# A three-layer kernel on one core: modulation by feature with six open banks at the start, and reordered joints with norm products on VectorE

## The chip, the core and the metric

The kernel runs on one core of one Trainium2 chip. The metric is the device time of one launch in microseconds, in which lower is better; a kernel's time is the median of its runs. Of the core's engines the text speaks of TensorE (matrix products and transposes; PE in rows), VectorE (DVE), ScalarE (ACT), GpSimd (POOL) and SyncE (SP), whose queue issues the loads from HBM into SBUF. PSUM holds the sums of TensorE in banks of 512 floats per partition.

## The reference

Three layers over a sequence of 1024 tokens of width 1024, with a context of 256 tokens beside it. The start and the two joints matter here:

```python
def layer(x, ctx, mod_x, mod_c, norm1_w, ...):            # first layer
    sh1, sc1, g1, sh2, sc2, g2 = jnp.split(mod_x[:, None, :], 6, -1)
    csh1, csc1, ... = jnp.split(mod_c, 6, -1)
    hx = modulate(rmsnorm(x, norm1_w), sh1, sc1)          # h * (1 + scale) + shift
    hc = modulate(rmsnorm(ctx, norm1_w), csh1, csc1)
    aq, ak, av, mq, mk, mv, mo, ... = mixer_inputs(hx, w_in, ...)   # hx @ w_in, split
    ...                                                   # attention, mLSTM, w_out
    x = x + g2 * expert_choice_ffn(hx2, w_router, w_gate, w_up, w_down)

def first_block(...):
    mod_x = jax.nn.silu(c) @ w_mod[l] + b_mod[l]
    mod_c = jax.nn.silu(c_ctx) @ w_mod[l] + b_mod[l]

def even_layer(x, norm_g, w_in, ...):                     # second layer
    z = rmsnorm_2(x, norm_g) @ w_in
    ...
    return x + jnp.concatenate([y_a, y_b], axis=-1) @ w_out

def odd_layer(x, norm_g, w_in, conv_w, w_out):            # third layer
    z = rmsnorm_2(x, norm_g) @ w_in
    ...
```

All is in float32. A product of matrices is made on TensorE from operands that are split in a high part (a cast on ScalarE) and a remainder, "lo" (a subtraction on VectorE or GpSimd), as three products: high by high, low by high, high by low.

## The kernel before

**The start** (`h_all`, `mod_early`, `kv_open`, `kv_tile`). x comes in eight tiles of 128 tokens. `normed` loads a tile, squares it on ScalarE (`norm_rows`, L230), makes the reciprocal root in tiny VectorE operations (L176 to L182) and scales the rows (L358). Eight TensorE transposes (L374) and two copies bring the tile into `xnT`, where partitions are features: eight "features" kt of 128 columns, each with 1024 tokens. `mod_early` makes shift and scale for both inputs, x and context: 16 loads of 512 KB of `wmod` through the `hi` and `lo` buffers, four matmuls for each (L298) with the two columns of silu(c), a sum over all eight kt, then copies, transposes (L306), bias and scale (L307, L312). `wmod` is laid out by input kt, so that every column of shift and scale is complete only with the last load of its group of eight. `finish` then makes the modulated high part `hxh` (ScalarE, L364) and the remainder `hxl` (VectorE, L365 and L136) for half of the tokens, and `kv_tile` multiplies a token tile by the key, value and gate columns `wkv` (24 matmuls of 272 columns into one bank of `mm`, L160 to L162) and copies the result out (L418 to L420). The context follows with two tiles.

**A unit** (`unit`, L1264) multiplies normed rows by weights with seven block products where eight would be plain (sums of weight blocks, `S`, on VectorE at L1212 to L1222; sums of row blocks in `norm_pair`). Its weights come through `operands`, which loads raw blocks ahead (`feed`); `raw` has six buffers in the even joint's stretch.

**The joint into the even layer** (L1421 to L1453). The last expert matmul ends, its rows are added into `xacc` in HBM, and the rows come back as four pairs of tiles, `ph` (t and t + 4). `norm_pair` squares them, scales by the reciprocal root and by the norm's row `nrow`, transposes four quarter blocks into the banks `s` and `o` (L1321), and makes the row sums and their splits, on which `unit(…, 0)` (pairs 0 and 1) and `unit(…, 1)` (pairs 2 and 3) work with 256-column products. The third call of `unit` has 512 columns. The first tile of a pair gets one VectorE operation (L1313); the second gets a ScalarE scaling (L1314) and a GpSimd product with the row (L1315).

**The joint into the odd layer** (L1478 to L1497) is the same with the rows `x` in SBUF: the even layer's last pass adds the output to `x` (L1393), token tiles in the order 0, 4, 1, 5, 2, 6, 3, 7, and calls `then(t)` behind each, which stores the tile and after tile 5 norms pair 0, after tile 7 pair 1.

Order: a scheduler sets the order of instructions on each engine from the order of the code and priorities; `high_priority` pulls a block ahead. Within an engine, and on SyncE's queue, an instruction that waits holds all behind it.

## Time and profile before

| what | value |
|---|---|
| median of the runs | 3333.42 us (3332.51 to 3335.74, 3 runs) |
| the profiled execution | 3336.12 us, its span 3334.3 us |
| mean granted TensorE clock of the span | 0.967 of full speed |
| TensorE busy | 3098.8 us, 93% of the span |
| VectorE, ScalarE, GpSimd busy | 2026.3, 1394.8, 1206.4 us |
| TensorE's share of the chain that ended last | 41% |
| loads and stores | 366.77 MB, 110 GB/s mean |

The share of busy time is a mean over stages. Where TensorE is busy all the time, other engines' work is hidden; where it waits, the row says for whom (`<-`): the engine and the tile that ended the wait last.

### The profile page before, as it was taken

To read this page: it belongs to the slowest core of one execution; us is meant where nothing else is said; L and a number is where in the kernel's file an instruction comes from. 1 tells how busy PE (TensorE), PEld (TensorE's weight loads), DVE (VectorE), ACT (ScalarE), POOL (GpSimd) and SP (SyncE) were. 2 spreads that over 40 slices of the span, in tenths; PEclk is the share of its full clock that TensorE was granted. 3 is DMA by queue.
4 is the path that set the end of the run, shared out by engine and by line. 5 is a ranking of instruction groups with operands and counts; after the bars stand their busy time and mean duration, and the time that the engine had idled before them with its cause. 6 is when DMAs were issued, how large, how long until landed. Compare 5 with 4: busy or idle time off the path is not lost. (4 is left out here: it accounts for less than half of the span.)

```text
span 3334.3 us, 43810 instructions
## 1 busy us (share of the span) xinstructions
PE 3098.8 (93%) x15829; PEld 2559.3 (77%) x15829; DVE 2026.3 (61%) x3879; ACT 1394.8 (42%) x2564; POOL 1206.4 (36%) x855
## 2 busy tenths in 40 slices
PE   6998988997999689999997999999999999999998
PEld 5986765775777577888785888888888888777787
DVE  5886678666999755455556455455455455444545
ACT  5645465444877542333314433333333333233312
POOL 0000000001332455455744434334334333666663
PEclk8998989998999899999998999999999999999999
DMA  5344223329999412221621111111111111211342
GB/s 199 96 138 129 62 75 115 98 96 392 371 378 366 111 39 73 76 70 64 205 82 63 47 45 51 45 48 48 45 51 45 47 49 45 69 64 64 110 149 76
DMA packets 142878, 366.77 MB, mean 110 GB/s; under 512 B 17299, under 2 KB 27059, under 8 KB 142661
## 3 DMA queue, kind: packets, MB, share of 16 engines
q1 hardware_dynamic: 137764, 346.14, 30.2%
q0 software_dynamic: 4896, 17.83, 2.1%
q8 instruction: 125, 2.05, 0.3%
q14 instruction: 93, 0.75, 0.1%
HBM read 311.43 MB, written 52.48 MB: 109 GB/s over the span
## 5 line engine op out<-in xcount | busy, mean ns | idle before, releaser
L1264 PE MATMUL ps_mm<-h,hi 128*128 128x512 f32 (+1 forms) x4272 | 1088.6, 394 | 44.7 <-ACT qk L1292 10.8
L1264 PEld LDWEIGHTS ps_mm<-h,hi 128*128 128x128 f32 x4272 | 784.2, 189 | 215.3 <-ACT qk L1292 17.2
L134 POOL TENSOR_TENSOR lo<-S,hi 128x512 fp32r<-128x512 f32 x302 | 402.9, 1337 | 586.9 <-PE ps_mm L1264 398.4
L1264 PE MATMUL ps_mm<-h,lo 128*128 128x512 f32 (+1 forms) x2136 | 566.6, 388 | 0.0
L1264 PEld LDWEIGHTS ps_mm<-h,lo 128*128 128x128 f32 x2136 | 399.7, 189 | 82.5
L134 POOL TENSOR_TENSOR lo<-raw,hi 128x512 fp32r<-128x512 f32 (+1 forms) x244 | 337.4, 1387 | 313.0 <-ACT hi L1196 232.8
L1196 ACT CAST hi<-S 128x512 fp32r<-128x512 f32 x302 | 187.1, 620 | 531.7 <-PE ps_mm L1264 510.9
L136 DVE TENSOR_TENSOR lo<-raw,hi 128x1024 fp32r<-128x1024 f32 (+1 forms) x218 | 285.0, 1330 | 35.5 <-ACT hi L148 31.7
L1196 ACT CAST hi<-raw 128x512 fp32r<-128x512 f32 x240 | 148.9, 622 | 369.5 <-PE ps_mm L1264 323.1
L148 ACT CAST hi<-raw 128x1024 fp32r<-128x1024 f32 (+1 forms) x222 | 230.8, 1050 | 96.0 <-PE ps_mm L162 60.7
L1217 DVE TENSOR_TENSOR S<-raw,raw 128x512 f32<-128x512 f32 x76 | 66.6, 877 | 202.7 <-POOL lo L134 201.5
L323 POOL MEMSET macc<- 128x512 f32 x8 | 4.2, 526 | 474.3 <-DMA mods<-macc 354.6
L160 PE MATMUL ps_mm<-hi,hxh 128*128 128x256 f32 (+1 forms) x448 | 131.6, 296 | 3.0 <-ACT hxh L364 2.8
L162 PE MATMUL ps_mm<-hi,hxl 128*128 128x256 f32 (+1 forms) x448 | 129.4, 292 | 2.4 <-DVE hxl L136 2.3
L161 PE MATMUL ps_mm<-lo,hxh 128*128 128x256 f32 (+1 forms) x448 | 130.8, 293 | 0.0
L1213 DVE TENSOR_TENSOR S<-S,raw 128x512 f32<-128x512 f32 x76 | 103.7, 1364 | 39.2 <-POOL lo L134 38.9
L161 PE MATMUL ps_mm<-lo,xT 128*128 128x512 f32 x256 | 105.3, 411 | 15.1 <-DVE lo L136 12.7
L1183 POOL TENSOR_TENSOR y<-y,g 128x1024 f32<-128x1024 f32 x15 | 40.2, 2679 | 198.9 <-ACT y L1179 178.7
L1294 DVE TENSOR_TENSOR qk<-ps_mm,pq 128x512 f32<-128x512 f32 (+1 forms) x75 | 69.1, 938 | 68.9 <-PE ps_mm L1264 68.6
L1745 DVE CUSTOM_DVE_ANT_0 P<-ps_s,bias 128x128 f32<-128x128 f32 (+1 forms) x192 | 61.8, 348 | 80.4 <-PE ps_s L1740 78.9
L160 PE MATMUL ps_mm<-hi,xT 128*128 128x512 f32 x256 | 103.8, 405 | 2.4 <-ACT hi L148 2.1
L1365 ACT CAST yh<-r 128x1024 fp32r<-128x1024 f32 x28 | 29.4, 1050 | 180.5 <-PE ps_s L161 168.5
(587 smaller groups left out, 6430.4 us busy)
## 6 DMA issues: line engine op xcount, KB each, us to landing
raw<-in_wexp_dram SPq DMA_DIRECT2D x192, 512.0 KB
raw<-in_wo_dram SPq DMA_DIRECT2D x228, 256.0 KB
mraw<-in_wmod_dram SPq DMA_DIRECT2D x64, 256.0 KB
raw<-in_we_dram SPq DMA_DIRECT2D x64, 256.0 KB
r<-ye SPq DMA_DIRECT2D x14, 512.0 KB
r<-in_weo_dram SPq DMA_DIRECT2D x14, 512.0 KB
r<-yo SPq DMA_DIRECT2D x14, 512.0 KB
r<-in_wo_dram SPq DMA_DIRECT2D x14, 512.0 KB
```

Of the source, the lines that this page charges most:

```text
L134: nc.gpsimd.tensor_sub(lo, raw, hi.bitcast(F32))
L136: nc.vector.tensor_sub(lo, raw, hi.bitcast(F32))
L148: self.nc.scalar.copy(hi, raw)
L160: nc.tensor.matmul(out, l[0], r[0], start=start, stop=False)
L161: nc.tensor.matmul(out, l[0], r[1], start=False, stop=False)
L162: nc.tensor.matmul(out, l[1], r[0], start=False, stop=stop)
L1196: self.nc.scalar.copy(hi, x)
L1213: nc.vector.tensor_sub(s2, s1, a11)
L1217: nc.vector.tensor_sub(s3, a11, a21)
L1264: nc.tensor.matmul(ps, w[a][:, kt * P:(kt + 1) * P], h[b][:, kt, cs], start=start and i == 0, stop=i == 11, skip_group_check=True)
L1294: self.nc.vector.tensor_add(dst, ps, add)
L1745: nc.vector.tensor_tensor_reduce(p, ps, bias[:, n - m:], op0=ALU.add, op1=ALU.max, scale=1.0, scalar=-3e38, accum_out=mx[:, j:j + 1])
```

## The change

It has three parts.

1. **Start.** The host lays `wmod`'s first two groups out by output feature (`wmodf`): two loads of 512 KB bring all inputs for the shift and the scale of one feature. `mod_sum(f)` sums them on TensorE with silu(c) in 32-column weights (`cpad`), `mod_cols(f, …)` turns the row into columns with two small products by a selector `sel`. So features get ready one by one. The key and value banks of six token tiles (three of `mm`, three of `g`) are opened together, and `step(kt, nxt)` adds feature kt to all six: modulation of tokens 0 to 768, the sums of feature `nxt` = kt + 2, 12 matmuls of the first two terms, `mod_cols(nxt)`, 6 matmuls of the third. Tiles 6 and 7 come in after steps 2 and 4, and their keys and values follow behind the six. The loads' and TensorE's order is written by hand (`manual_schedule`). x tiles take other buffers (`X2`, `hi`, `lo`, three of `hx`).
2. **Norm products.** Both tiles of a pair get the VectorE operation; `norm_pair` becomes a generator with a stop between norm and transposes.
3. **Joints.** Even: on SyncE `nrow` and the eight first raw loads go ahead of the ph loads, pairs 0 and 1 are normed before either is transposed, pairs 2 and 3 are loaded and normed ahead of unit 0. Odd: pairs 0 to 3 are normed after tiles 4, 5, 6 and 7 and pairs 0 and 1 transposed after 6 and 7; the odd output weights' first four raw blocks are loaded at tile 0 (`self.early`).

```diff
-    def mod_early(self):
...
+    def mod_open(self):
...
+        self.cpad = self.t("cpad", [KT, 32])
+        nc.gpsimd.memset(self.cpad, 0.0)
+        nc.vector.tensor_copy(self.cpad[:, :, 0:2], self.csil.rearrange("p a k -> p k a"))
+        self.sel = self.t("sel", [2])
+        nc.vector.tensor_reduce(self.sel, self.ident.rearrange("p (j x) -> p x j", j=4)[:, 0:2], axis=AX.X, op=ALU.add)
...
+    def mod_load(self, f):
+        self.wm[f] = [self.t("X", [4, 256], name="wm") for _ in range(2)]
+        for h in range(2):
+            self.nc.sync.dma_start(self.wm[f][h].rearrange("p a b -> p (a b)"), self.A["wmodf"][f][:, h * D:(h + 1) * D])
+    def mod_sum(self, f):
+        nc = self.nc
+        ps = self.pt("tr")
+        for h in range(2):
             for j in range(4):
+                nc.tensor.matmul(ps[32 * j:32 * j + 32, :256], self.cpad[:, 4 * h + j], self.wm[f][h][:, j],
+                                 start=h == 0, stop=h == 1, tile_position=(0, 32 * j))
+        return ps
+    def mod_cols(self, f, ps):
+        nc = self.nc
+        row = self.t("hrow", [2, P])
+        nc.scalar.copy(row.rearrange("p a b -> p (a b)"), ps[:, :256])
+        pw = self.pt("tr")
+        for i in range(2):
+            nc.tensor.matmul(pw[:, 2 * i:2 * i + 2], row[:, i], self.sel, start=True, stop=True)
+        nc.vector.tensor_add(self.modc.rearrange("p a (i f) -> p f i a", i=2)[:, f], pw[:, 0:4].rearrange("p (i a) -> p i a", i=2),
+                             self.col("bmod")[:, 0:16].rearrange("p (i f) -> p f i", i=2)[:, f, :, None].to_broadcast([P, 2, 2]))
+        nc.vector.scalar_tensor_tensor(self.sc1[:, :, f], self.modc[:, :, 8 + f], 1.0, self.col("n1")[:, f:f + 1].to_broadcast([P, 2]),
+                                       op0=ALU.add, op1=ALU.mult)
...
+        spare = [self.t("hx", [D], name="xin") for _ in range(3)]
         self.hx = ([self.t("hx", [D], F32R, "hxh") for _ in range(KT)], [self.t("hx", [D], F32R, "hxl") for _ in range(KT)])
...
+        xt, self.wm, self.pre = {}, {}, []
+        self.mod_open()
+        with self.tc.manual_schedule(engines={nc.sync.engine, nc.tensor.engine}):
+            def loads(text):
+                for what in text.split():
+                    i = int(what[1])
+                    if what[0] == "x":
+                        xt[i] = rows("x", i, tile=spare[i - 5] if i > 4 else None,
+                                     tag=("xin", "xin", "X2", "hi", "lo")[min(i, 4)])
...
+                    elif what[0] == "m":
+                        self.mod_load(i)
...
+                        self.pre.append(self.wraw(A["wkv"][i]))
+            def part(f):
+                self.mod_cols(f, self.mod_sum(f))
+            def step(kt, nxt):
+                for s in (slice(0, 512), slice(512, 768)):
+                    finish(self.hx[0][kt][:, s], self.hx[1][kt][:, s], xnT[:, kt, s], kt, 0)
+                sums = self.mod_sum(nxt) if nxt < KT else None
+                for t in range(6):
+                    self.kv_part(ps[t], t, kt, (0, 1))
+                if sums is not None:
+                    self.mod_cols(nxt, sums)
+                for t in range(6):
+                    self.kv_part(ps[t], t, kt, (2,))
+            loads("x0 x1 m0 x2 x3 w0 m1 x4 x5 w1 m2")
+            tile_in(0)
+            tile_in(1)
+            part(0)
+            self.wkv = self.wpair(A["wkv"])
+            tile_in(2)
+            tile_in(3)
+            part(1)
+            tile_in(4)
+            tile_in(5)
+            ps = [self.pt(("mm", "g")[t // 3]) for t in range(6)]
+            loads("m3")
+            step(0, 2)
+            loads("x6 m4")
+            step(1, 3)
+            loads("m5")
+            step(2, 4)
+            tile_in(6)
+            loads("x7 m6")
+            step(3, 5)
+            loads("m7")
+            step(4, 6)
+            tile_in(7)
+            self.pre += [self.wraw(A["wcv"][0][i]) for i in range(2)]
+            step(5, 7)
+            step(6, 8)
+            step(7, 8)
         self.kv_open()
+        for t in range(6):
+            self.kv_out(ps[t], t)
+        s = slice(768, 1024)
+        for kt in range(KT):
+            finish(self.hx[0][kt][:, s], self.hx[1][kt][:, s], xnT[:, kt, s], kt, 0)
+        for t in (6, 7):
+            self.kv_tile(t)
+        hc = [self.t("X", [4, 256], F32R, "hc") for _ in range(4)]
+        self.hc = ([hc[k // 4][:, k % 4, :] for k in range(KT)], [hc[2 + k // 4][:, k % 4, :] for k in range(KT)])
+        ts = normed([rows("ctx", t) for t in range(2)])
         for kt in range(KT):
             ps = self.pt("tr")
...
+    def kv_part(self, ps, t, kt, terms=(0, 1, 2)):
+        hx = self.hx if t < 8 else self.hc
+        s = slice(t % 8 * P, t % 8 * P + P)
+        for i in terms:
+            self.nc.tensor.matmul(ps[:, :272], hx[i == 2][kt][:, s], self.wkv[i == 1][kt], start=kt == i == 0,
+                                  stop=kt == KT - 1 and i == 2)
+    def kv_out(self, ps, t):
...
+        def load(i, j):
+            if self.early:
+                return self.early.pop(0)
+            return self.wraw(srcs[i][:, j * 512:(j + 1) * 512]) if i < n else None
...
     def feed(self, srcs, tiles):
-        pairs = [(x[:, 0], x[:, 1]) for x in (self.spare(t) for t in tiles)]
+        pairs = [(x[:, 0], x[:, 1]) for x in tiles]
...
-        nc.vector.scalar_tensor_tensor(xn[0], xs[0], rs[:, 0:1], row, op0=ALU.mult, op1=ALU.mult)
-        nc.scalar.mul(xn[1], xs[1], rs[:, 1:2])
-        nc.gpsimd.tensor_mul(xn[1], xn[1], row)
+        for i in range(2):
+            nc.vector.scalar_tensor_tensor(xn[i], xs[i], rs[:, i:i + 1], row, op0=ALU.mult, op1=ALU.mult)
+        yield
         ps = {}
         for n, bank in zip(("11", "12", "22", "21"), banks):
...
         out("T2", t2, "pool")
         out("B21", ps["21"], "dve")
         out("T4", t4, "pool")
+        yield
...
-            self.feed([A["we7"][i // 5 * 4 + i % 5 - 1] if i % 5 else self.wf[i // 5] for i in range(20)], ("q", "q", "s"))
-            row = self.t("s", [D], name="nrow")
-            nc.sync.dma_start(row, A["en"].to_broadcast([P, D]))
-
-            def norm(t):
+            def load(t):
                 x = xs[t] if t < 2 else two("ph")
                 for i in range(2):
                     nc.sync.dma_start(x[i], self.xacc[(t + 4 * i) * P:(t + 4 * i + 1) * P, :])
...
+                return self.norm_pair(t, x, row, T, ("s", "o", "s", "o"))
+            def step(*ts):
                 with self.tc.high_priority(offset=100):
-                    self.norm_pair(t, x, row, T, ("s", "o", "s", "o"))
-
-            norm(0)
-            norm(1)
+                    for t in ts:
+                        next(n[t])
+            with self.tc.manual_schedule(engines={nc.sync.engine}):
+                pairs = [self.spare(t) for t in ("q", "q", "s")]
+                row = self.t("s", [D], name="nrow")
+                nc.sync.dma_start(row, A["en"].to_broadcast([P, D]))
+                self.feed([A["we7"][i // 5 * 4 + i % 5 - 1] if i % 5 else self.wf[i // 5] for i in range(20)], pairs)
+                n = [load(t) for t in range(2)]
+            step(0, 1, 0, 1)
+            n += [load(t) for t in (2, 3)]
+            step(2, 3)
             for a in tl:
                 nc.gpsimd.memset(a[:, 0:16], 0.0)
             self.unit(self.put2(tl, 16), None, 0)
-            norm(2)
-            norm(3)
+            step(2, 3)
             self.unit(self.put2(tl, 16, 1), None, 1)
...
-                def norm(t):
+                n = [self.norm_pair(t, [self.xs[t], self.xs[t + 4]], row, lambda i: self.t("T", [512]), ("s",) * 4)
+                     for t in range(4)]
+                def step(*ts):
                     with self.tc.high_priority(offset=100):
-                        self.norm_pair(t, [self.xs[t], self.xs[t + 4]], row, lambda i: self.t("T", [512]), ("s",) * 4)
+                        for t in ts:
+                            next(n[t])
...
                 def then(t):
+                    if t == 0:
+                        self.early = [self.wraw(A["wo7"][0][:, j * 512:(j + 1) * 512]) for j in range(4)]
                     nc.sync.dma_start(self.x3d[t * P:(t + 1) * P, :], self.xs[t])
-                    if t in (5, 7):
-                        norm((t - 5) // 2)
+                    if t in (4, 5):
+                        step(t - 4)
+                    elif t > 5:
+                        step(t - 6, t - 4)
                 self.out_sums(A["weo"], self.ye, [((15,), (0, 4, 1, 5, 2, 6, 3, 7), then)], ("o",))
-                self.feed([A["wo7"][i] for i in range(56)], ("X",) * 3)
+                self.feed([A["wo7"][i] for i in range(56)], [self.spare("X") for _ in range(3)])
                 self.qk = [self.t("qk", [D]) for _ in range(2)]
                 self.unit(self.put2(self.qk), None, 0)
-                norm(2)
-                norm(3)
+                step(2, 3)
                 self.unit(self.put2(self.qk, 0, 1), None, 1)
...
-    a["wmod"] = np.stack([chunk(wm[:, j * D:(j + 1) * D]) for j in range(6)])
+    a["wmod"] = np.stack([chunk(wm[:, j * D:(j + 1) * D]) for j in range(2, 6)])
+    a["wmodf"] = np.stack([chunk(np.concatenate([wm[:, i * D + k * P:i * D + k * P + P] for i in range(2)], 1)) for k in range(8)])
```

Three places show what this moves. **TensorE, end of the modulation**, before (`hi`, `lo` hold `wmod` and then `wkv`, `ps_mm` the banks):

```order
L298 MATMUL ps_mm_394<-lo_425,csil 2x256 x4
L298 MATMUL ps_mm_394<-hi_431,csil 2x256 x4
L298 MATMUL ps_mm_394<-lo_437,csil 2x256 x4
L374 MATMUL ps_tr_237<-ident,xin_224 128x128 x4
L374 MATMUL ps_tr_243<-ident,xin_224 128x128 x4
L306 MATMUL ps_g_449<-ident,hrow_443 128x128
L306 MATMUL ps_g_452<-ident,hrow_443 128x128
L160 MATMUL ps_mm_513<-hi_460,hxh_93 128x272
L161 MATMUL ps_mm_513<-lo_461,hxh_93 128x272
L160 MATMUL ps_mm_541<-hi_460,hxh_93 128x272
```

and now (`wm` holds a feature's weights, `ps_mm` and `ps_g` the six banks, `hxh_96` is feature 0):

```order
L387 MATMUL ps_tr_329<-ident,xin_93 128x128 x4
L387 MATMUL ps_tr_335<-ident,xin_93 128x128 x4
L310 MATMUL ps_tr_359<-wm_147,cpad_115 32x256 x4
L310 MATMUL ps_tr_359<-wm_148,cpad_115 32x256 x4
L490 MATMUL ps_mm_341<-hi_217,hxh_96 128x272
L490 MATMUL ps_mm_341<-lo_218,hxh_96 128x272
L490 MATMUL ps_mm_342<-hi_217,hxh_96 128x272
L490 MATMUL ps_mm_342<-lo_218,hxh_96 128x272
L490 MATMUL ps_mm_343<-hi_217,hxh_96 128x272
L490 MATMUL ps_mm_343<-lo_218,hxh_96 128x272
```

The sums of one feature stand directly ahead of the products of another, and a feature is used in six banks before the next one comes.

**SyncE's queue, even joint**, before (`wf` and `we` are the unit's raw weights, `xacc` the rows, `en` the norm's row):

```order
L140 DMA raw_10841<-in_we_dram 128x512
L140 DMA raw_10843<-in_we_dram 128x512
L1432 DMA ph_10826<-xacc 128x1024
L1432 DMA ph_10827<-xacc 128x1024
L1432 DMA ph_10828<-xacc 128x1024
L1432 DMA ph_10829<-xacc 128x1024
L140 DMA raw_10863<-in_we_dram 128x512
L140 DMA raw_10875<-in_we_dram 128x512
L140 DMA raw_11243<-in_we_dram 128x512
L140 DMA raw_11245<-in_we_dram 128x512
L1427 DMA nrow_10879<-in_en_dram 128x1024
L140 DMA raw_11305<-in_we_dram 128x512
```

and now:

```order
L1540 DMA nrow_10911<-in_en_dram 128x1024
L140 DMA raw_10913<-wf 128x512
L140 DMA raw_10915<-wf 128x512
L140 DMA raw_10917<-wf 128x512
L140 DMA raw_10919<-wf 128x512
L140 DMA raw_10921<-in_we_dram 128x512
L140 DMA raw_10923<-in_we_dram 128x512
L140 DMA raw_10943<-in_we_dram 128x512
L140 DMA raw_10955<-in_we_dram 128x512
L1518 DMA ph_10902<-xacc 128x1024
L1518 DMA ph_10903<-xacc 128x1024
L1518 DMA ph_10904<-xacc 128x1024
```

The norm's row moved from behind the ph loads to the head, and the last two of eight raw loads moved ahead of the ph loads.

**VectorE, odd joint, pairs 2 and 3** (`pq` and `qk` are the sums of unit 0's products, `T` and `h` the row sums and remainders), before:

```order
L1294 TENSOR_TENSOR qk_15923<-ps_mm_15926,pq_15979 128x256
L1294 TENSOR_TENSOR qk_15923<-ps_mm_15925,pq_15979 128x256
L1294 TENSOR_TENSOR qk_15922<-ps_mm_15926,pq_15953 128x256
L176 TENSOR_SCALAR rst_16027<-ss_16021 128x2
L178 RECIPROCAL rst_16027<-rst_16027 128x2
L179 TENSOR_TENSOR rst_16027<-rst_16027 128x2
L180 TENSOR_TENSOR rst_16027<-rst_16027 128x2
L181 TENSOR_SCALAR rst_16027<-rst_16027 128x2
L182 TENSOR_TENSOR ss_16022<-rst_16027 128x2
L1313 SCALAR_TENSOR_TENSOR x_3074_14419<-x_3074_14419,ss_16022,row_15639 128x1024
L176 TENSOR_SCALAR rst_16087<-ss_16081 128x2
L178 RECIPROCAL rst_16087<-rst_16087 128x2
```

and now:

```order
L182 TENSOR_TENSOR ss_15890<-rst_15895 128x2
L1429 TENSOR_TENSOR T_15962<-ps_s_15942,T_15948 128x512
L1306 TENSOR_TENSOR S_16287<-raw_15989,raw_16011 128x512
L1403 SCALAR_TENSOR_TENSOR x_3100_14494<-x_3100_14494,ss_15890,row_15714 128x1024
L1403 SCALAR_TENSOR_TENSOR x_3101_14495<-x_3101_14495,ss_15890,row_15714 128x1024
L176 TENSOR_SCALAR rst_15976<-ss_15970 128x2
L136 TENSOR_TENSOR h_15702<-ps_s_15937,h_15701 128x4x128
L136 TENSOR_TENSOR h_15700<-ps_s_15942,h_15699 128x4x128
L178 RECIPROCAL rst_15976<-rst_15976 128x2
L179 TENSOR_TENSOR rst_15976<-rst_15976 128x2
L180 TENSOR_TENSOR rst_15976<-rst_15976 128x2
L181 TENSOR_SCALAR rst_15976<-rst_15976 128x2
```

The norm of pair 2 moved ahead of unit 0's sums, between the remainders of pair 1, and a second product with `row` follows the first.

## Rows read from the trace of the kernel before

**Rows 1.** page, part 1: busy us, share of the span, instructions

```profile
PE 3098.8 (93%) x15829; PEld 2559.3 (77%) x15829; DVE 2026.3 (61%) x3879; ACT 1394.8 (42%) x2564; POOL 1206.4 (36%) x855
```

**Rows 2.** by stretch: engines' busy us (instructions), clock, DMA share, GB/s

```profile
0.00:10.00 10.00, 0.88 (x8) 0.14 (x8) 1.86 (x9) 5.17 (x8) 0.71 (x6) 1.00 0.78 272
...
20.00:30.00 10.00, 6.85 (x50) 2.68 (x50) 3.90 (x18) 4.92 (x12) 0.32 (x1) 0.54 1.03 416
...
60.00:70.00 10.00, 9.86 (x80) 9.64 (x79) 7.61 (x19) 7.10 (x13) 0.00 (x0) 1.00 0.17 52
```

**Rows 3.** waits of TensorE, 0 to 120 us: total us, times, longest

```profile
PE ps_mm L298 <- DMA hi<-in_wmod_dram: 15.0, 4, 9.1
```

**Rows 4.** TensorE by time, start: start us, us, instruction, count, [idle before]

```profile
31.37 0.61 PE L298 MATMUL ps_mm<-lo,csil 128*2 128x256 f32 x8
...
36.36 1.03 PE L298 MATMUL ps_mm<-lo,csil 128*2 128x256 f32 x8 [1.94 <-DMA lo<-in_wmod_dram]
...
43.72 0.59 PE L160 MATMUL ps_mm<-hi,hxh 128*128 128x272 f32 x1 [2.75 <-ACT hxh L364]
```

**Rows 5.** ScalarE in order of time, end of the start

```profile
89.91 0.44 ACT L418 COPY kc<-ps_mm 128x128 f32<-128x128 f32 x2 [2.23 <-PE ps_mm L162]
```

**Rows 6.** ScalarE by line and shape, to 100 us: busy us, mean ns

```profile
L364 ACT ACTIVATE hxh<-xnT,modc,sc 128x512 fp32r<-128x512 f32 x16 | 11.7, 803 | 1.1 <-DVE sc L312 1.0
```

**Rows 7.** VectorE by line and shape, 0 to 100 us

```profile
L136 DVE TENSOR_TENSOR hxl<-tmp,hxh 128x512 fp32r<-128x512 f32 x16 | 10.5, 688 | 0.0
L365 DVE TENSOR_SCALAR tmp<-xnT,sc,modc 128x512 f32<-128x512 f32 x16 | 8.2, 543 | 0.0
```

**Rows 8.** TensorE in order of time, even joint

```profile
1149.68 1.09 PE L1321 MATMUL ps_s<-ident,ph 128*128 128x128 f32 x4 [24.81 <-DVE ph L1313]
...
1158.82 1.79 PE L1264 MATMUL ps_mm<-h,hi 128*128 128x256 f32 x7 [1.24 <-DVE h L136]
...
1175.50 0.68 PE L1321 MATMUL ps_s<-ident,ph 128*128 128x128 f32 x4 [4.26 <-DVE ph L1313]
1178.72 1.11 PE L1321 MATMUL ps_o<-ident,ph 128*128 128x128 f32 x4 [2.54 <-POOL ph L1315]
...
1188.11 1.10 PE L1264 MATMUL ps_mm<-h,hi 128*128 128x256 f32 x7 [1.31 <-DVE h L136]
...
1195.96 1.32 PE L1264 MATMUL ps_mm<-h,hi 128*128 128x512 f32 x5
```

**Rows 9.** SyncE's queue in order of time, even joint

```profile
1132.33 1.94 SPq L1432 DMA_DIRECT2D ph<-xacc  x4
...
1140.50 0.42 SPq L1427 DMA_DIRECT2D nrow<-in_en_dram  x1
```

**Rows 10.** VectorE in order of time, even joint

```profile
1126.89 7.59 DVE L1217 TENSOR_TENSOR S<-raw,raw 128x512 f32<-128x512 f32 x1
...
1142.68 0.16 DVE L182 TENSOR_TENSOR ss<-rst 128x2 f32<-128x2 f32 x1
...
1148.26 2.47 DVE L1313 SCALAR_TENSOR_TENSOR ph<-ph,ss,nrow 128x1024 f32<-128x1024 f32 x2
```

**Rows 11.** TensorE in order of time, odd joint

```profile
1794.30 1.11 PE L1321 MATMUL ps_s<-ident,x 128*128 128x128 f32 x4 [6.09 <-DVE h L136]
...
1820.70 0.77 PE L1321 MATMUL ps_s<-ident,x 128*128 128x128 f32 x4 [4.26 <-DVE x L1313]
1823.92 1.97 PE L1321 MATMUL ps_s<-ident,x 128*128 128x128 f32 x8 [2.45 <-POOL x L1315]
...
1834.78 1.86 PE L1264 MATMUL ps_mm<-h,hi 128*128 128x256 f32 x7 [0.72 <-DVE h L136]
...
1843.68 1.55 PE L1264 MATMUL ps_mm<-h,hi 128*128 128x512 f32 x6
```

**Rows 12.** VectorE in order of time, odd joint

```profile
1787.27 0.68 DVE L1393 TENSOR_TENSOR x<-x,ps_o 128x512 f32<-128x512 f32 x1
...
1788.62 2.25 DVE L1313 SCALAR_TENSOR_TENSOR x<-x,ss,row 128x1024 f32<-128x1024 f32 x1
```

## Prediction before the run

> **What bounds the kernel now.** I read the engines' shares first: TensorE is busy 93% of the span [rows 1], so most of the program runs at TensorE's own pace, and an edit off that path is worth nothing. The edits touch three stretches where TensorE is not at that pace: the start (0 to 90 us), the joint into the even layer (1124 to 1196 us) and the joint into the odd layer (1781 to 1844 us). I read each by itself: busy time by stretch, then TensorE's waits and its instructions in order of time, then the engine that released them.
>
> In the start the loads run at 272 GB/s in the first 10 us and at 416 later [rows 2]. TensorE has little to do meanwhile: from 20 to 30 us it is 6.85 us busy, at a mean granted clock of 0.54, near the lower of its two levels (1.2 GHz). Its longest wait is for the tiles of `wmod`, 15.0 us in 4 waits [rows 3]. The last `wmod` sum begins at 36.36 [rows 4]; only behind it can any column of shift and scale be made, and the first key and value product starts at 43.72, after 2.75 us of waiting for ScalarE's first modulated tile. From 60 us TensorE runs 80 matmuls in 10 us, 0.125 us each, at a clock of 1.00 [rows 2]. The context's keys are copied out at 89.91 [rows 5]; behind that the program goes on as before, so I measure the start by that row.
>
> In the even joint TensorE idles 24.81 us until the first normed pair is there, and later 4.26 us for VectorE's product of the second half and 2.54 us for GpSimd's [rows 8]. The odd joint looks the same: 6.09, then 4.26 and 2.45 us [rows 11].
>
> **The change part by part. Start.** The stream up to the third feature's weights is six x tiles and two context tiles (0.52 MB each), two `wkv` tiles (0.56) and three features (1.05 each): 8.5 MB with the small constants. 2.7 MB arrive by 10 us; the rest at 416 GB/s takes 14 us, so the last bytes land at 24 us at best. The first step cannot start before: its first instructions on TensorE are the sums of feature 2. I take 26.5.
>
> A step is 18 matmuls of 0.125 us (2.25), eight sums in two groups of 0.61 (1.22) [rows 4] and two small ones that turn rows into columns (0.2, an estimate, since a 272-column one is 0.125): 3.7 us. Beside it VectorE has a 512-wide modulation and remainder, 0.54 + 0.69 [rows 7], and about half of that again for the 256-wide ones, 2.2 us with the columns; ScalarE has 0.80 [rows 6], its half and a copy. So TensorE bounds a step if the loads hold. The four weight buffers hold two features, and each reload is released by the sums two steps ahead: a load of 2.5 us at 416 GB/s, its latency and an x tile now and then have 7.4 us. That fits, with little left.
>
> Eight steps are 29.6 us. I give 2 us to the lower clock at their beginning, and 1 us each to the transposes of tiles 6 and 7. The six banks close at 26.5 + 29.6 + 2 + 2 = 60.1. Then come 48 matmuls for tiles 6 and 7 (6.0 us), whose modulation (eight 256-wide slices on VectorE) hides only in part, 2 us; 16 context transposes (2 us), 48 matmuls (6.0). And here is a wait that key products used to cover: the context's norm and modulation now stand behind the copies out of the banks on ScalarE and VectorE, with no other work left on TensorE: 1 to 3 us, I take 2. That is 78.1; I take 77, since the first of tile 6's products can run under the last slices. 77 is 13 us before 89.91. Bounds: 18 us if the steps begin at 24 at the full clock and nothing is uncovered, 2 if every step waits for its load.
>
> **Even joint.** The ph loads were issued at 1132.33 and `nrow` only at 1140.50, behind four raw loads and their waits for buffers [rows 9]. The row came last: the first pair's reciprocal root was there at 1142.68 + 0.16, its product began at 1148.26 [rows 10]. Now `nrow` goes first. But two raw loads that stood behind the ph loads stand ahead of them now, and their buffers come free when VectorE's sum of L1217 ends, at 1126.89 + 7.59 = 1134.48 [rows 10]; four ph loads are queued behind that on SP and go out at about 1134.9, 2.5 us later. Issue to root took 10.5 us, so the root is there at 1145.4 and two products of 1.24 end at 1147.9: TensorE starts some 2 us before 1149.68. The second pair's products end by 1151.4. From there to the second unit's first operand VectorE has 24 half-row sums and remainders (0.69 [rows 7]), four products, five quarter-size sums (0.4, an estimate from the same row) and a dozen tiny ones (0.16 in [rows 10]): 16.6 + 5.0 + 2.0 + 2.0 = 25.6, so 1177. It was 1188.11 [rows 8]. TensorE's own sum says the same: unit 0 took 12.4 us (1158.82 to 1175.50 less its wait of 4.26), 32 transposes take 5.4 to 8.7 (0.68 or 1.09 for four). Gain 11, so the 512-wide unit begins at 1185, not 1195.96; what ends late then is VectorE. What can uncover the cost: ScalarE's squares of the third pair now stand ahead of casts of the first, so if that pair's loads are late, the first unit waits with them, 2 to 4 us. Bounds 4 and 15.
>
> **Odd joint.** Nothing is loaded here but the row. The pairs start a tile earlier, and pairs 2 and 3 are normed under unit 0 and not after it, so the waits of 4.26 and 2.45 us and the slow transposes around them go [rows 11]. VectorE bounds: its last addition began at 1787.27 [rows 12], and with one product more ahead of it ends near 1789. To the second unit's first operand it then has 19 sums and remainders (13.1), six products (7.4), four operand sums of weights (2.8), five quarter-size ones (2.0) and 18 tiny ones (2.9): 28.2, so 1817, and 1818.5 with some waiting, against 1834.78 [rows 11]. TensorE has less than that there (12.4 + 5.4 us to the same point). Gain 16, the 512-wide unit at 1827.5; bounds 10 and 20.
>
> **Norm products.** They are inside these sums: each adds 1.24 us to VectorE and takes a multiplication off ScalarE and one off GpSimd. VectorE instructions on two SBUF tiles are stretched at times: L1217 to 7.59 us [rows 10], a product to 2.25 [rows 12]. The Trainium skill (SBUF — State Buffer, section Who interferes with whom) says that a VectorE instruction with two SBUF inputs contends with a GpSimd instruction that reads SBUF, and that issue order decides who is blocked. By that rule the added products are of the very kind that can be held, which speaks against this edit; what it would cost is the second rival. The two stretched rows agree with it.
>
> The rest of the program keeps its instructions; loads that change places in other stages I put at 0, within 2 us either way.
>
> **Sum.** 13 + 11 + 16 = 40 us. The profiled execution of before took 3336.12 us, of which 3334.3 are its span; that is 2.7 above the median of the runs. So 3296 in a profile, 3293 as the median.
>
> **The rivals.** *The loads pace the start.* For it: the whole stream of the start is 14.9 MB, which at 416 GB/s cannot end before 39 us, and the weight buffers are two features deep. Against it: 2.5 us of load stand against 3.7 us of step. It would leave 2 of the 13 us: 3304.
> *GpSimd holds the added products.* Eight products each pay 1.0 us more (2.25 less 1.24 [rows 10, 12]), and the remainders queued behind them on VectorE pay with them; with 4 us for squares that wait for late ph loads, 12 of the joints' 27 us go: 3305. For it: VectorE is what I expect to be late next. Against it: GpSimd loses four multiplications per joint, and its queue is shorter.
> *TensorE stays at 1.2 GHz (slower than before).* Place: the eight steps and the first two units of both joints, whose work now comes in smaller pieces with waits between. At the lower level a matmul is 0.25 us; a step is 6.5 (18 of these and the sums at some 1.0 a group), 52 us from 26.5, and 28 more for tiles 6 and 7 and the context: the start ends at 106.5, 17 us late. A unit would lose 10 us, four of them 40, more than the 27 the joints gain. Together 30 us slower: 3363. It decides if the granted clock from 30 to 60 us stays near 0.5; in the old start it was 1.00 once matmuls ran without gaps [rows 2], so I hold it unlikely.
> *The first two together*: 3316.
>
> **How the numbers follow.** Forecast 0.62 (by itself 3283 to 3300), loads 0.14, products 0.14, these two together 0.06, half clock 0.04. A measurement of this kernel can tell about 0.2% (6.7 us) from no change; of the two together I give 0.02 to a gain within that. Faster 0.94, same 0.02, slower 0.04. The range begins where all three parts gain their most (18 + 15 + 20 = 53 us, 3280) and ends at 3313, above each single rival and below the two together.
>
> **What would show it.** Right: the first key products near 27 us, steps 3.7 us apart, a granted clock above 0.9 from 35 us, the context copy near 77. The ph loads go out some 10 us after the last expert matmul, TensorE idles there 22 to 23 us, no later wait in the joint is over 2 us, and the 512-wide unit begins 60 us after the last expert matmul, not 71. In the odd joint the 512-wide unit begins some 38 us after the last addition, not 56. Wrong: a wait for `wm` above 1 us in every step; many products above 2 us; a granted clock of 0.5 through the units; a new wait in a stage that the change does not touch.

## The result and the profile after

The changed kernel takes 3307.94 us (median of 4 runs, 3305.60 to 3310.66), the kernel before 3334.58 beside it (4 runs): ratio 0.9915, interval 0.9901 to 0.9928. By these medians it is 26.6 us faster, by the ratio 28.3; forecast were 40. The time lies in the range, but 15 us above the forecast, where two of the rivals had theirs (3304 and 3305), so the terms have to be gone through.

The profile after, span and clock of the core:

```profile
core 0: 3305.9 us, clock 0.972
```

I cut the program at four marks that both traces have: the copy of the context's keys on ScalarE, the end of the last expert matmul, the first 512-wide matmul of the even layer's units (`ps_mm<-h,hi`, 128x512), and the same in the odd layer. Times in us from the span's start.

| | before | after | gain to here |
|---|---|---|---|
| context keys copied | 89.91 | 83.47 | 6.4 |
| last expert matmul ends | 1124.86 | 1112.32 | 12.5 |
| even 512-wide unit begins | 1195.96 | 1177.19 | 18.8 |
| odd 512-wide unit begins | 1843.68 | 1814.22 | 29.5 |
| span | 3334.3 | 3305.9 | 28.4 |

By the terms of the sum: start 12.5 (forecast 13, though only 6.4 of it where I looked for it), even joint 71.10 to 64.87, 6.2 (11), odd joint from the first x transpose 62.28 to 50.52, 11.8 (16), and 2.1 lost in what lies between and after the joints (0). Each figure is from one profile. Kernels below whose even joint has the same source lie up to 2.2 us apart there (63.55 to 65.75), those with the same odd joint up to 1.5 (50.51 to 52.01), s3 apart, so a difference of less than some 2 us is not shown by one mark alone.

**Start.** Busy time by stretch (us; PE, PEld, DVE, ACT, POOL with instructions; then TensorE's granted clock, DMA share, GB/s), against [rows 2]:

```profile
20.00:30.00 10.00, 7.41 (x41) 5.29 (x40) 8.39 (x24) 6.03 (x12) 0.00 (x0) 0.50 0.90 329
30.00:40.00 10.00, 9.90 (x99) 7.57 (x98) 7.83 (x25) 6.13 (x12) 0.00 (x0) 0.98 0.72 251
```

TensorE in order of time there (start, length, instruction; in brackets the idle time before it and what ended it), against [rows 4]:

```profile
17.22 1.01 PE L321 MATMUL ps_tr<-sel,hrow 128*128 128x2 f32 x4 [1.81 <-ACT hrow L318]
18.09 1.95 PE L387 MATMUL ps_tr<-ident,xin 128*128 128x128 f32 x8
21.58 1.94 PE L387 MATMUL ps_tr<-ident,xin 128*128 128x128 f32 x8 [1.54 <-DVE rst L176]
23.45 1.94 PE L310 MATMUL ps_tr<-wm,cpad 128*32 128x256 f32 x16
26.44 1.01 PE L321 MATMUL ps_tr<-sel,hrow 128*128 128x2 f32 x4 [1.05 <-ACT hrow L318]
27.31 3.60 PE L387 MATMUL ps_tr<-ident,xin 128*128 128x128 f32 x16
31.01 1.07 PE L310 MATMUL ps_tr<-wm,cpad 128*32 128x256 f32 x16
32.01 0.39 PE L490 MATMUL ps_mm<-hi,hxh 128*128 128x272 f32 x1
...
34.92 1.07 PE L310 MATMUL ps_tr<-wm,cpad 128*32 128x256 f32 x16
```

The first step begins at 31.01, not at 26.5, and what stands before it is not a load: from 10 us on no wait of TensorE ends with one, and from 15 to 31 us none of ScalarE or VectorE either. Between 20 and 30 us TensorE is 7.41 us busy at a granted clock of 0.50 (1.2 GHz) with transposes and sums of 1.94 us a group, and waits in between for ScalarE's row copy and VectorE's root: each x tile goes in turn through VectorE, TensorE and ScalarE. From there the steps are 3.91 us apart.

Behind the steps the context, on ScalarE. The second row here is the copy of tile 6's and 7's keys, the last the context's:

```profile
65.78 1.06 ACT L230 ACTIVATE junk<-xin 128x1024 bf16<-128x1024 f32 x1 [2.33 <-DVE hxl L136]
...
69.69 0.43 ACT L496 COPY kx<-ps_mm 128x128 f32<-128x128 f32 x2 [1.29 <-PE ps_mm L490]
...
72.39 1.02 ACT L377 ACTIVATE hc<-ps_tr,modc,sc 128x256 fp32r<-128x256 f32 x2 [2.26 <-PE ps_tr L466]
...
83.47 0.43 ACT L496 COPY kc<-ps_mm 128x128 f32<-128x128 f32 x2 [1.98 <-PE ps_mm L490]
```

What TensorE does between these two copies (69.70 to 83.45) besides the context's 48 products is 16 transposes, with one wait for VectorE's scaled rows, and 24 products of the next stage's weights with `hc`, nearly all of which stand ahead of the last key product (groups: busy us, mean ns of one | idle before):

```profile
L466 PE MATMUL ps_tr<-ident,xin 128*128 128x128 f32 x16 | 2.7, 281 | 1.8 <-DVE xin L371 1.8
L160 PE MATMUL ps_mm<-hi,hc 128*128 128x256 f32 x8 | 2.2, 281 | 0.0
```

**Even joint**, TensorE in order of time, against [rows 8]: the idle stretch behind the experts is 21.54 us, not 24.81; unit 0's first product begins at 1144.76, 32.4 us after the last expert matmul as in the kernel before, the third pair's second tile comes late (1155.11), and unit 1's first full product starts only at 1169.50.

```profile
1111.93 0.39 PE L162 MATMUL ps_mm<-hi,aT 128*128 128x512 f32 x1
1133.86 1.09 PE L1410 MATMUL ps_s<-ident,ph 128*128 128x128 f32 x4 [21.54 <-DVE ph L1403]
...
1144.76 2.59 PE L1353 MATMUL ps_mm<-h,hi 128*128 128x256 f32 x8 [0.98 <-ACT h L1416]
...
1155.11 1.11 PE L1410 MATMUL ps_s<-ident,ph 128*128 128x128 f32 x4 [1.54 <-DVE ph L1403]
...
1169.50 1.10 PE L1353 MATMUL ps_mm<-h,hi 128*128 128x256 f32 x7 [1.28 <-DVE h L136]
...
1177.19 1.09 PE L1353 MATMUL ps_mm<-h,hi 128*128 128x512 f32 x4
```

VectorE between, against [rows 10]: the same kinds of instruction quiet (to 1136.25) and beside GpSimd (from 1146.13). A pair of products takes 2.48 or 3.96 us, an operation on two numbers 0.16 or 1.2. GpSimd's rows stand below them.

```profile
1131.83 0.16 DVE L180 TENSOR_TENSOR rst<-rst 128x2 f32<-128x2 f32 x1
1132.03 0.17 DVE L181 TENSOR_SCALAR rst<-rst 128x2 f32<-128x2 f32 x1
...
1132.43 2.48 DVE L1403 SCALAR_TENSOR_TENSOR ph<-ph,ss,nrow 128x1024 f32<-128x1024 f32 x2
...
1146.87 1.20 DVE L180 TENSOR_TENSOR rst<-rst 128x2 f32<-128x2 f32 x1
1148.10 1.21 DVE L181 TENSOR_SCALAR rst<-rst 128x2 f32<-128x2 f32 x1
...
1151.10 3.96 DVE L1403 SCALAR_TENSOR_TENSOR ph<-ph,ss,nrow 128x1024 f32<-128x1024 f32 x2
```

```profile
1146.77 1.29 POOL L134 TENSOR_TENSOR h<-g,h 128x512 fp32r<-128x512 f32 x1
1148.01 1.28 POOL L134 TENSOR_TENSOR h<-PT,h 128x512 fp32r<-128x512 f32 x1
```

The two small operations end at 1148.07 and 1149.31, GpSimd's two subtractions at 1148.06 and 1149.29: each small operation is held until its neighbour's instruction ends. From 1130.2 to 1144.3 GpSimd does nothing, and there the same operations take 0.16.

**Odd joint**, TensorE, against [rows 11]: the waits of 6.09, 4.26 and 2.45 us have become 8.14 and 2.64. In the 8.14 us four small operations of VectorE took 3.4 (0.80, 0.75, 0.71 and 1.18), where 0.65 is their quiet time.

```profile
1777.97 1.11 PE L1410 MATMUL ps_s<-ident,x 128*128 128x128 f32 x4 [8.14 <-DVE x L1403]
...
1785.80 0.58 PE L1353 MATMUL ps_mm<-h,hi 128*128 128x256 f32 x1 [2.64 <-ACT h L1416]
...
1814.22 1.09 PE L1353 MATMUL ps_mm<-h,hi 128*128 128x512 f32 x4
```

### The profile page after: what moved, and what is told of

It reads as the page before. It is cut to its first block, busy times and chain, and to the rows that moved or that the text cites. A ratio compares the mean times of both kernels' runs of the same rounds, so it can differ in the third digit from the quotient of the medians.

```text
span 3305.9 us, 43866 instructions
## 1 busy us (share of the span) xinstructions
PE 3084.2 (93%) x15857; PEld 2552.1 (77%) x15857; DVE 2034.8 (62%) x3915; ACT 1385.7 (42%) x2564; POOL 1186.9 (36%) x846
## 4 chain that ended last, share of the span: by engine, by line
PE 75%; DVE 10%; DMA 7%; ACT 4%; issue 3%; POOL 1%; SPq 0%; DVEq 0%; ACTq 0%; POOLq 0%
PE ps_mm L1353 42%; PE ps_mm L161 4%; PE ps_mm L162 4%; PE ps_mm L160 4%; PE ps_o L1918 2%; DVE lo L136 2%; DMA raw<-in_wexp_dram 2%; PE ps_s L1845 2%; PE ps_s L162 1%; PE ps_s L160 1%; PE ps_s L161 1%; ACT hi L148 1%; PE ps_s L1901 1%; PE ps_tr L1033 1%; PE ps_O L1040 1%
## 5 line engine op out<-in xcount | busy, mean ns | idle before, releaser
L1306 DVE TENSOR_TENSOR S<-raw,raw 128x512 f32<-128x512 f32 x76 | 59.7, 786 | 202.9 <-POOL lo L134 201.7
L161 PE MATMUL ps_mm<-lo,xT 128*128 128x512 f32 x256 | 104.6, 409 | 15.6 <-DVE lo L136 14.2
L161 PE MATMUL ps_mm<-lo,hxh 128*128 128x256 f32 x384 | 111.2, 290 | 0.0
L162 PE MATMUL ps_mm<-hi,hxl 128*128 128x256 f32 x384 | 111.0, 290 | 0.0
L160 PE MATMUL ps_mm<-hi,hxh 128*128 128x256 f32 x384 | 110.5, 290 | 0.0
```

The source lines that it names most:

```text
L160: nc.tensor.matmul(out, l[0], r[0], start=start, stop=False)
L161: nc.tensor.matmul(out, l[0], r[1], start=False, stop=False)
L162: nc.tensor.matmul(out, l[1], r[0], start=False, stop=stop)
```

## Experiments

All marks of all kernels, each from its own profile (us). "Even" is from the last expert matmul to the 512-wide unit, "odd" from the first x transpose to the 512-wide unit, "unit to unit" from the one 512-wide unit to the other.

| kernel | median, ratio [95%] | context copy | expert end | even | odd | unit to unit |
|---|---|---|---|---|---|---|
| before | | 89.91 | 1124.86 | 71.10 | 62.28 | 647.7 |
| after | 3307.94, 0.9915 [0.9901, 0.9928] | 83.47 | 1112.32 | 64.87 | 50.52 | 637.0 |
| s1_start | 3321.01, 0.9958 [0.9944, 0.9971] | 85.31 | 1111.64 | 69.46 | 61.46 | 646.1 |
| s2_even | 3329.77, 0.9982 [0.9973, 0.9991] | 90.53 | 1123.48 | 63.55 | 61.81 | 648.3 |
| s3_odd | 3328.07, 0.9978 [0.9969, 0.9987] | 89.78 | 1122.30 | 70.17 | 54.29 | 640.7 |
| s4_norm | 3333.30, 0.9995 [0.9986, 1.0004] | 91.05 | 1123.98 | 69.10 | 61.57 | 645.5 |
| c1_oldprod | 3308.16, 0.9904 [0.9886, 0.9922] | 86.47 | 1109.20 | 64.60 | 55.96 | 641.4 |
| c2_tiny | 3295.32, 0.9869 [0.9852, 0.9885] | 86.71 | 1111.31 | 62.55 | 47.58 | 631.2 |
| c3_ctx | 3311.40, 0.9918 [0.9901, 0.9935] | 84.63 | 1115.17 | 65.75 | 52.01 | 637.8 |
| c4_wkv | 3306.46, 0.9913 [0.9896, 0.9930] | 84.87 | 1110.28 | 65.40 | 50.51 | 637.2 |
| c5_pool | 3303.32, 0.9900 [0.9883, 0.9916] | 83.63 | 1110.46 | 66.76 | 51.04 | 635.5 |
| c6_act | 3330.99, 0.9991 [0.9981, 1.0000] | 84.61 | 1109.99 | 64.60 | 47.75 | 639.7 |
| c8_ph | 3301.02, 0.9901 [0.9884, 0.9917] | 87.10 | 1110.70 | 62.86 | 50.53 | 635.7 |
| c7_best | 3321.92, 0.9959 [0.9944, 0.9973] | 86.27 | 1113.76 | 57.15 | 51.68 | 641.4 |

### One part of the change at a time

Each kernel is the one before with one part of the diff ahead of the prediction: s1 the whole of the start and nothing else, s2 the even joint with its order and its second product on VectorE, s3 the same for the odd joint, s4 the old orders with only this, in both joints:

```diff
-        nc.vector.scalar_tensor_tensor(xn[0], xs[0], rs[:, 0:1], row, op0=ALU.mult, op1=ALU.mult)
-        nc.scalar.mul(xn[1], xs[1], rs[:, 1:2])
-        nc.gpsimd.tensor_mul(xn[1], xn[1], row)
+        for i in range(2):
+            nc.vector.scalar_tensor_tensor(xn[i], xs[i], rs[:, i:i + 1], row, op0=ALU.mult, op1=ALU.mult)
```

> The kernel before with the new start alone; both joints stay as they were. In the trace of the changed kernel the context keys are copied out 6.4 us earlier than before, but the last expert matmul ends 12.5 us earlier, so some 6 us more come from the stretch between, whose code is the same. Theory A (the start also shifts what follows it, by the order and the loads that it leaves behind): this kernel is 11 to 14 us faster than before, about 3322, and its last expert matmul is 12 us earlier. Theory B (the 6 us belong to the run or to the other edits): it is 6 us faster, about 3328, and its last expert matmul 6 us earlier.

Measured: 14.0 us faster by the ratio (before took 3336.4 beside it). The context's copy comes 4.6 us earlier, the last expert matmul 13.2. So more than half of the start's worth appears behind the stage that was changed, with neither joint touched. Much of it appears in the head and attention stage. Busy time from 450 to 510 us, before and then s1_start (columns as above):

```profile
450.00:510.00 60.00, 52.49 (x278) 40.22 (x278) 51.67 (x207) 39.83 (x118) 0.53 (x1) 0.77 0.15 45
```

```profile
450.00:510.00 60.00, 51.19 (x309) 38.34 (x310) 51.73 (x216) 42.36 (x116) 0.00 (x0) 0.89 0.10 32
```

309 matmuls instead of 278 in the same 60 us, at a clock of 0.89 instead of 0.77, though the two windows do not hold quite the same piece of work. All ten kernels with the new start show 0.87 to 0.90 there, the four with the old one 0.77 to 0.80. The source of that stage is the same; the schedule is not: TensorE's order differs in dozens of places. That the other order raises the clock is argued, not shown, since no kernel here has the old start with the new order.

> The kernel before with the even joint alone (order of loads and norms, both products on VectorE there); start and odd joint as before. Theory A (the parts add up, and the joint is worth what the changed kernel's trace shows between the last expert matmul and the 512-wide unit, 65.0 us against 71.1): 6 us faster, about 3328.5. Theory B (the joint gains the 11 us that I forecast, and the changed kernel lost part of it only together with the other edits): about 3323.5.

Measured: 6.0 us faster by the ratio, 7.6 in the joint itself. That is theory A; the 11 us are not there when the joint stands alone either.

> The kernel before with the odd joint alone (order of norms, early raw loads, both products on VectorE there). Theory A (parts add up; in the changed kernel the 512-wide unit begins 42.4 us after the last addition, 56.4 before, of which 2 are lost ahead of that addition): 11 to 12 us faster, about 3323. Theory B (the 16 us that I forecast are there when the joint stands alone): about 3318.5.

Measured: 7.3 us faster by the ratio, 8.0 in the joint. That is neither theory: two thirds of the 11.8 us of the changed kernel. The joint's source is the changed kernel's, the new products too, so no run explains the 3.8 us between them.

> The kernel before with nothing but the second product of each pair moved from ScalarE and GpSimd to VectorE; all orders as before. Theory A (the waits of 2.5 us for GpSimd's product go, and where GpSimd's subtractions run, VectorE's new products are stretched, but none ends later than GpSimd's did): 2.5 us in the even joint and 3 to 4 in the odd one, 5 to 7 us faster, about 3328.5. Theory B (the products are held by GpSimd long enough to take that back): within 2 us of before, with products of 2 to 4 us in the trace.

Measured: no difference that the runs can tell; the joints are 2.0 and 0.7 us shorter, no more than such a mark scatters. By their ratios s1, s2 and s3, which hold s4's products in their joints, sum to 14.0 + 6.0 + 7.3 = 27.3 us, and the whole has 28.3: the parts neither help nor hinder one another much.

### What the joints pay for

c1 is the changed kernel with the old product of a pair's second tile (ScalarE, then GpSimd). c2 leaves the refinement of the reciprocal root out of the norms of both joints: the root is ScalarE's alone. c1:

```diff
-        for i in range(2):
-            nc.vector.scalar_tensor_tensor(xn[i], xs[i], rs[:, i:i + 1], row, op0=ALU.mult, op1=ALU.mult)
...
+        nc.scalar.mul(xn[1], xs[1], rs[:, 1:2])
+        nc.gpsimd.tensor_mul(xn[1], xn[1], row)
```

and c2:

```diff
-        self.norm_rows(xs, rs, ss)
...
+        nc.vector.tensor_scalar(v, ss, 1.0 / D, EPS, op0=ALU.mult, op1=ALU.add)
+        nc.scalar.activation(v, v, AF.Sqrt)
+        nc.vector.reciprocal(rs, v)
```

> The changed kernel with the second product of each pair back on ScalarE and GpSimd, all new orders kept. Theory A (the product on VectorE pays in the new order as well: GpSimd's product takes 2.3 us against 1.24 and stands in the queue of its subtractions): the even joint (last expert matmul to the 512-wide unit, 64.9 us in the changed kernel) gets 2 to 4 us longer and the odd one (first transpose to the 512-wide unit, 50.5 us) 3 to 6, some 7 us slower, about 3315. Theory B (VectorE is the bound of the new joints, so 5 us less of products on it in each gives time back): both joints 1 to 3 us shorter, about 3304.

Measured: the total can't be told from that of the changed kernel. The even joint is as long (64.60), the odd one 5.4 us longer; unit to unit it is 4.4. So in the new order the VectorE products are worth nothing in the even joint and 4 to 5 us in the odd. What the total can hide it with stands in the table: in this kernel's profile the experts end 3.1 us earlier (1109.20), in a stretch that the edit does not touch.

> The changed kernel without the refinement of the reciprocal root in the joints' norms: four tiny VectorE operations of 2 elements a partition less per pair (L179 to L182); the roots are then a little less exact, and that part of the computation is left out. Theory A (each of these operations can be held until a GpSimd operation ends, 0.7 to 1.24 us instead of 0.16, and that is where the joints' missing gain went): the even joint 3 to 4 us shorter than 64.9, the odd one 3 to 5 shorter than 50.5, about 3301. Theory B (they cost their own 0.2 us, and the stretch goes over to the next operation in line): each joint 1 us shorter or less, about 3306.

Measured: 0.9869 against 0.9915, the fastest of all kernels and faster than the changed one beyond both intervals, with 2.3 us less in the even joint and 2.9 in the odd one (5.9 from unit to unit). That lies between the theories: more than the 1 us of B in each joint, less than the 3 of A. Sixteen operations on two numbers are taken off VectorE in each joint; undisturbed they are 16 x 0.16 = 2.6 us. In the even joint the small operations fall from 7.6 to 2.5 us, but the products rise from 11.4 to 11.8; in the odd one they fall from 10.4 to 1.3, and the products rise from 12.4 to 15.6. So a part of the price goes over to the next operation in line, as B says. That they are long there can be read from the groups by line, all four norms of the even joint, in the kernel before and after (busy us, mean ns of one):

```profile
L182 DVE TENSOR_TENSOR ss<-rst 128x2 f32<-128x2 f32 x4 | 2.8, 707 | 0.1
L179 DVE TENSOR_TENSOR rst<-rst 128x2 f32<-128x2 f32 x4 | 2.6, 646 | 0.1
L181 DVE TENSOR_SCALAR rst<-rst 128x2 f32<-128x2 f32 x4 | 1.8, 441 | 0.1
L178 DVE RECIPROCAL rst<-rst 128x2 f32<-128x2 f32 x4 | 0.7, 166 | 2.1 <-ACT rst L177 2.1
```

```profile
L1403 DVE SCALAR_TENSOR_TENSOR ph<-ph,ss,nrow 128x1024 f32<-128x1024 f32 x8 | 11.4, 1465 | 0.1
L180 DVE TENSOR_TENSOR rst<-rst 128x2 f32<-128x2 f32 x4 | 1.7, 420 | 0.1
L178 DVE RECIPROCAL rst<-rst 128x2 f32<-128x2 f32 x4 | 0.6, 158 | 0.8 <-ACT rst L177 0.8
```

Added up over the six lines, these operations take 7.6 us in the changed even joint and 10.4 in the odd one, where 24 of 0.16 would be 3.8; the products 11.4 and 12.4 where eight of 1.24 would be 9.9. So the operations on two numbers take 3.8 and 6.6 us more than in quiet, the large products 1.5 and 2.5; that all of it is for GpSimd is read from rows such as those above, not measured one by one.

### Where the start's last microseconds are

c3 writes the context's norm behind the last step, ahead of the copies out of the six banks. c4 writes the split (cast and remainder) of the second half of the key and value weights behind the first step; its load stays where it was in SyncE's queue (10.27 us, 10.83 in the changed kernel). c3:

```diff
+        ts = normed([rows("ctx", t) for t in range(2)])
...
-        ts = normed([rows("ctx", t) for t in range(2)])
```

and c4:

```diff
-            self.wkv = self.wpair(A["wkv"])
+            half = [self.wchunk(A["wkv"][0], 4)]
...
+            half.append(self.wchunk(A["wkv"][1], 4))
```

> The changed kernel with the norm of the two context tiles written ahead of the copies out of the six banks. In the changed kernel ScalarE's first square of the context waits 2.33 us for a buffer that it shares with the modulation of the last slices, and the scaled rows are there at 71.9, 2.2 us after the last key product of tile 7. Theory A (this wait is on the path): the context keys are copied out 2 to 3.5 us earlier than 83.47, about 3305. Theory B (the context's modulation, between TensorE, ScalarE and VectorE in turn, bounds the stretch): less than 0.7 us.

> The changed kernel with the split of the second half of wkv (features 4 to 7) written behind the first step. In the changed kernel its cast of 1.08 us stands on ScalarE ahead of the copy of the second feature's sums, TensorE waits 1.05 us for that copy, and the transposes of x tiles 4 and 5 wait behind it. Theory A (this chain sets the first step at 31.0): the first step's sums begin 1 to 2 us earlier, and the context keys as much, about 3306.5. Theory B (the step waits for the rows of tile 5 and their own chain at the lower clock): under 0.5 us.

Measured: neither total can be told from that of the changed kernel. But c3 does shorten its stretch, ScalarE's copies of tile 6's and 7's keys and of the context's:

```profile
72.71 0.43 ACT L496 COPY kx<-ps_mm 128x128 f32<-128x128 f32 x2 [5.90 <-PE ps_mm L490]
...
84.63 0.43 ACT L496 COPY kc<-ps_mm 128x128 f32<-128x128 f32 x2 [2.23 <-PE ps_mm L490]
```

That is 11.9 us, against 13.8 in the changed kernel, c1, c2 and c4, and TensorE's wait of 1.8 us is gone: theory A for that stretch. The mark at 84.63 hides it, because in this execution the copies out of the six banks came 3.3 us later (65.60 against 62.33), at a granted clock of 0.72 from 55 to 60 us against 1.00.

c4 tests less than it was made for: the scheduler left the cast ahead of the copy of the second feature's sums (22.86 and 23.95 on ScalarE). Its first step's sums do come 2.1 us before the changed kernel's 31.01:

```profile
28.92 1.93 PE L310 MATMUL ps_tr<-wm,cpad 128*32 128x256 f32 x16
```

But the eight other kernels with this start, which lack this edit, have them at 28.84 to 29.72, so this is no effect of the edit; it is the changed kernel's profile that is late. Its granted clock was 0.56 from 15 to 30 us, 0.59 to 0.84 in the others.

### Other places for the same small operations

c5 gives the norms' small operations to GpSimd:

```diff
-        self.norm_rows(xs, rs, ss)
+        self.norm_rows(xs, rs, ss, nc.gpsimd)
```

> The changed kernel with the small operations on the 2 sums of the joints' norms (scale, root with its refinement) on GpSimd's queue instead of VectorE's; everything else as in the changed kernel. Theory A (VectorE's small operations are long because GpSimd runs beside them, 0.70 to 1.24 us each where one takes 0.16 us alone, and this lies on the chain of both joints): each joint 1.5 to 2.5 us shorter than in the changed kernel (even 64.9 us, odd 50.5 us), total about 3303 us. Theory B (the length of these operations is beside the path, or the chain then waits behind GpSimd's own additions and products in its queue): joints equal or up to 4 us longer, total 3308 to 3316 us.

Measured: the even joint 1.9 us longer, the odd one 0.5, but from unit to unit 1.5 shorter. GpSimd in order of time, third pair of the even joint:

```profile
1150.10 0.21 POOL L179 TENSOR_TENSOR rst<-rst 128x2 f32<-128x2 f32 x1
1150.25 1.30 POOL L134 TENSOR_TENSOR h<-g,h 128x512 fp32r<-128x512 f32 x1
...
1152.74 0.21 POOL L180 TENSOR_TENSOR rst<-rst 128x2 f32<-128x2 f32 x1
```

Each takes only 0.2 us, but between two of them stand remainders of 1.30. For the even joint that speaks for theory B, by a difference no larger than the scatter; the odd joint stays unclear. The total, 3303 us, can't be told from that of the changed kernel.

c6 gives all of them but the reciprocal to ScalarE, with a new constant for the biases:

```diff
+            self.ecol = self.cpool.tile([P, 2], F32, name="ecol")
...
+        nc.scalar.activation(v, ss, AF.Identity, scale=1.0 / D, bias=self.ecol[:, 0:1])
+        nc.scalar.activation(s, v, AF.Sqrt)
+        nc.vector.reciprocal(s, s)
...
```

> The changed kernel with scale, root and refinement of the joints' norms on ScalarE as 8 small operations, and only the reciprocal on VectorE. Theory A (the price is VectorE being held while GpSimd runs): the even joint 2 us and the odd joint 2 to 3 us shorter than in the changed kernel (64.9 and 50.5 us), total about 3303 us. Theory B (it is the number of steps in a row, whichever engine has them, some 0.2 to 0.3 us each on ScalarE plus its queue): both joints within 1 us of the changed kernel, total 3307 to 3309 us.

Measured: the even joint 64.60 (B), the odd one 47.75, 2.8 us shorter (A). The total fits neither: 23 us above the changed kernel. None of it is in the joints. Between them this kernel loses 5.4 us, and from the odd 512-wide unit to the end 21.7, and the groups by line say where (after, then c6_act; busy us, mean ns of one):

```profile
L1353 PE MATMUL ps_mm<-h,hi 128*128 128x512 f32 x4144 | 1065.5, 397 | 37.7 <-ACT qk L1381 10.8 <-DVE pq L1370 8.4 <-ACT vc L1381 4.4
L1353 PE MATMUL ps_mm<-h,lo 128*128 128x512 f32 x2072 | 555.2, 391 | 0.0
```

```profile
L1353 PE MATMUL ps_mm<-h,hi 128*128 128x512 f32 x4144 | 1084.7, 401 | 33.4 <-ACT qk L1381 10.8 <-ACT dc L1381 4.5 <-ACT db L1381 4.5
L1353 PE MATMUL ps_mm<-h,lo 128*128 128x512 f32 x2072 | 566.8, 396 | 0.0
```

A 512-wide product of the units takes about 5 ns more in the mean, 19.2 + 11.6 = 30.8 us in all. About 9 us of that lie between the two 512-wide units; without them unit to unit would be 630.7, an estimate, close to c2's 631.2. In every other kernel here the two rows are 1065 to 1067 and 554 to 555; in c7 they are 1084.6 and 567.0. What only c6 and c7 have is `ecol`, a new constant of two columns. By the addresses in the programs it moves the units' weight tiles `hi` and `lo` up by 32 bytes, from starts of 32 beyond a multiple of 64 to multiples of 64; the other operand `h` stays where it was. That this is the cause is argued from that coincidence; no run moved the tiles alone.

c8 issues the first two pairs' ph loads two raw loads earlier, by a count in `wraw`. These loads bring the rows `ph` back from `xacc`; the expectations of c8 and c7 call them the head's weights, which they are not:

```diff
+                    if left[0] == 0:
+                        n.extend(load(t) for t in range(2))
...
-                n = [load(t) for t in range(2)]
```

> The changed kernel with the first two loads of the head's weights issued two raw loads earlier in the queue, ahead of the 7th and 8th raw load of the step before. Theory A (TensorE's idle stretch at the even joint is set by these loads, issued 8.5 us after the last expert matmul): the even joint 2 to 2.5 us shorter than 64.9 us, total about 3305.5 us. Theory B (the two raw loads that now come later are needed just as soon, or the loads wait for the same buffers): even joint within 0.7 us, total unchanged.

Measured: the even joint 2.0 us shorter, as by theory A, though that is no more than such a mark scatters, and the total, 3301 us, can't be told from the changed kernel's (0.9901 against 0.9915, the intervals overlap). That the loads go out earlier is plain: 7.05 us after the last expert matmul (1110.70), 8.5 in the changed kernel. SyncE's queue and then TensorE:

```profile
1117.75 1.75 SPq L1518 DMA_DIRECT2D ph<-xacc  x4
```

```profile
1128.95 1.08 PE L1410 MATMUL ps_s<-ident,ph 128*128 128x128 f32 x4 [18.25 <-DVE ph L1403]
...
1138.96 1.12 PE L1410 MATMUL ps_s<-ident,ph 128*128 128x128 f32 x4 [6.09 <-DVE ph L1403]
```

The first wait is 3.3 us shorter than in the changed kernel, and 1.3 of that is given back on the way to the 512-wide unit: TensorE now waits 6.09 us for the second pair.

c7 has c8's loads and a norm of one ScalarE root and one reciprocal:

```diff
+        nc.scalar.activation(v, ss, AF.Sqrt, scale=1.0 / D, bias=self.ecol[:, 0:1])
+        nc.vector.reciprocal(rs, v)
```

> The changed kernel with the scaling of the joints' norms folded into ScalarE's root, no refinement of the root (this part of the computation is left out in the joints), only the reciprocal on VectorE, and the first two loads of the head's weights two raw loads earlier. Theory A (holds on VectorE and these loads are separate prices of the joints): even joint about 60 us, odd joint 46 to 47 us, total 3290 to 3294 us. Theory B (VectorE without the refinement is all there is to be had): as without the refinement alone, 62.6 and 47.6 us, total about 3295 us.

Measured: the even joint 57.15, 7.7 us shorter and better than A. The odd one is 51.68, no shorter than the changed kernel's 50.52; from unit to unit, less 9.1 us of longer products, it would be 632.3, an estimate, 4.7 shorter and no better than c2. The total of 3321.9 has the same 31 us of longer products in it. Taking all of them off gives about 3291, in the band of A; but outside the joints this kernel is only 20.7 us longer than the changed one, which gives 3301. Both are estimates, and which holds is not shown. So the shorter even joint is real; A is not shown for the odd joint or the total.

## Why the prediction was right or wrong, point by point

**First step at 26.5: wrong, 31.0.** The step that failed is that the first step waits for bytes. It waits for a chain: six tiles one after another through VectorE's scaling, TensorE's transposes and ScalarE's copies, with two earlier features' sums between. The lower clock is a part of it: I had 0.54 in [rows 2] and charged 2 us for it behind the first step, not ahead of it. c4's profile shows how large a part at most: there the clock is 1.00 from 15 to 25 us (0.59 in the changed kernel), TensorE is busy 5.17 of these 10 us and VectorE 8.85, and the first sums still begin only at 28.92. So no more than some 2 of the 4.5 us go with the clock; that the rest is the chain's own length is argued. The rival that the loads pace the start fell: from 10 us on no wait of TensorE in the start ends with a load.

**Steps of 3.7 us, clock above 0.9: right.** They are 3.9 apart at 0.98 to 1.00. The rival of the half clock fell with it for the steps. In the joints the clock was low in part, in the kernel before too: 0.64 from 1144.76 to 1157 and 0.50 from 1778 to 1785.8 in the changed kernel, 0.50 from 1794 to 1807 in the one before.

**The uncovered context: mis-sized.** From the copies of tiles 6 and 7 (69.69) to the context's copy it took 13.8 us, where I had 2 + 6 + 2. The wait that I had named was about right: TensorE waits 1.8 us for the scaled rows and 0.5 for `hc`. (The waits of ScalarE in the rows above are others: that of 2.33 lies ahead of this stretch, and that of 1.98 is ScalarE waiting for the last products.) What the sum left out are the 24 products of the next stage that stand among the key products (three groups, of which one is shown above), some 2.8 us at 0.12 us from one to the next; the kernel before has them there as well. The transposes took 2.6 instead of 2. The whole start against 78.1: first step +4.5, steps -1.7, tiles 6 and 7 -1.1, context +3.7.

**"Behind that the program goes on as before": wrong, in my favour.** The copy gained 6.4 of the 13 us; another 6.1 came by the end of the experts, where I had put 0 within 2 us. All ten kernels with the new start end the experts at 1109 to 1115, the four with the old one at 1122 to 1125, though the copy is at 83 to 87 against 90 to 91. So the term of 13 came out as 12.5 for a reason that I did not give, and that stays open: that it was so near was luck.

**Even joint 11: mis-sized, 6.** Its front was nearly right: ph loads 8.5 us after the last expert matmul, TensorE idle 21.54, the second pair's products done 26.4 us after it (forecast 26.5). But unit 0's first product is no earlier than before, 32.4 us after the last expert matmul in both. The term that was mis-sized is VectorE's from there on: forecast 25.6 us, it took 30.8 (1138.64 to 1169.4). The 24 half-row sums took less than forecast, 14.4 for 16.6; the small operations took 5.6 for 2.0, the products 6.4 for 5.0, and waits 2.2 for which the sum had nothing. The tiny operations had been put at 0.16 and products at 1.24 from quiet rows [rows 10]. In the same joint of the kernel before, the groups above show 0.44 to 0.71 us for three of the six lines, and I did not read them. The trace before has the hold itself: I took the row `nrow` to come last ahead of VectorE's first product at 1148.26 [rows 10], but `nrow` was there at 1145.98, when GpSimd began its own product with it, and VectorE stood until 1148.26 in an operation on two numbers:

```profile
1145.99 2.35 DVE L182 TENSOR_TENSOR ss<-rst 128x2 f32<-128x2 f32 x1
```

It ends with GpSimd's product (1145.98, 2.34 us long).

**Odd joint 16: mis-sized, 12**, by the same term: 42.4 us from the last addition, not 38. Of the 14.0 us by which this is shorter than 56.4, 3.3 were given back ahead of the addition, so unit to unit has 10.7. From the addition's end to unit 1's operand it took 34.3 us, forecast 29.5; there the small operations took 8.2 for 2.9, the products 9.9 for 7.4. The largest wait is the 8.14 us for a norm of which VectorE's small operations are a part. c2, which takes most of them away, gives back 2.3 and 2.9 us of the 4.8 and 4.2 that the joints lack; for the rest no run has a cause.

**Norm products inside these sums.** They had no gain of their own in the forecast. s4 finds none that can be told in the old order; in the new one c1 finds nothing in the even joint and 4 to 5 us in the odd.

**The rival that GpSimd holds the added products** has a time (3305) closer to the result than my forecast, and the right engine, but not its mechanism: the products took 4.0 us more in both joints, the small operations 10.4. By the Trainium skill (SBUF — State Buffer, section Who interferes with whom) two SBUF inputs, or `tensor_scalar` in a mode that takes both ports, contend with GpSimd; the trace agrees, with L180 at 1.20 and L181 at 1.21 beside it, 0.16 and 0.17 without it, and additions with an input in PSUM at 0.67 to 0.69 throughout.

**The sum** was 40; 28.4 came in the profile: 0.5 short in the start (by two errors against each other), 4.8 and 4.2 in the joints, and 2.1 in the stages between.

## What to carry to other kernels

Cost an instruction by the mean of its group in the stretch where it will stand, not by one undisturbed row: 0.16 us became 0.7 to 1.2 when GpSimd ran beside it, whatever its size, so few operations in a chain matter more than small ones. Ask of an earlier start what chain of engines stands ahead of it, and what clock they have then. Follow a sum of TensorE's work through its queue, since products of another stage may stand in it. When a constant is added, look at the long loops too: in both kernels with the new constant, products that the change never touched took 31 us more, though the cause was not isolated.

## What the runs showed of the hardware

In the changed kernel VectorE operations on two numbers took up to 1.24 us beside GpSimd's 1.3 us remainders, in the kernel before 2.35 beside its product of 2.34, and 0.16 when GpSimd was idle; where rows were laid side by side, they ended with GpSimd's instruction. The reciprocal, 0.15 to 0.17, was held in no run. And two rows of 512-wide products moved from 397 and 391 to 401 and 396 ns in the two kernels whose weight tiles lie 32 bytes further on; no run moved the tiles alone.
